# A decoder layer on one core: later loads and stores around job u, key parts a piece later, and one head's probabilities scaled by ScalarE

## The chip, the core and the metric

The kernel runs on one core of a Trainium2 chip. The core has a matrix engine (TensorE, PE in the profile; its weight loads are PEld), VectorE (DVE), ScalarE (ACT), GpSimd (POOL) and SyncE (SP). Each engine takes its instructions from its own queue in the order in which the program gives them. Transfers between the chip's memory and the core's buffer are issued here by SP (the weights and inputs) and by POOL (all else), and run on 16 shared DMA engines. The metric is the time of one execution on the device in microseconds (us), smaller is better, as the median of several runs.

## The reference

One layer of a decoder over 512 positions of 2048 channels, in float32:

```python
h = rms_norm(x, norm_g[l])
proj = h @ w_in[l]
q, kv, g_logits, z_a, uv, z_b, merge_logits = jnp.split(proj, SPLIT_IDX, axis=-1)
o_a = nsa_attention(q, k_c, v_c, k_s, v_s, k_w, v_w, g_logits, ...) * jax.nn.silu(z_a)
o_b = spatial_gating(uv, ln_v_g[l], ln_v_b[l], sgu_w[l], sgu_b[l]) * jax.nn.silu(z_b)
g_a, g_b = jnp.split(jax.nn.sigmoid(merge_logits), 2, axis=-1)
merged = g_a * (o_a @ w_up_a[l]) + g_b * (o_b @ w_up_b[l])
x = x + merged @ w_out[l]
x = x + jax.nn.sigmoid(x @ w_ple_gate[l]) * (p[l] @ w_ple[l])
```

The attention has 16 heads in 4 groups and three branches (compressed, selected, window), each a softmax with a linear bias, weighted by a sigmoid gate and added. With 512 positions the selected and the window branch both see all earlier positions. The gating mixer is `u * (tril(W_s) LN(v) + b)`, with `u` and `v` the two halves of `gelu(uv)`. A final RMS norm follows.

## The kernel before

**Products in three parts.** Every float32 operand of a matrix product is held as a high part (rounded by ScalarE, `high`, L142 and L144) and a low part (the remainder, formed by VectorE, `low`, L148 and L150). A product is three matmuls: high by high, high by low, low by high. So every weight tile that SP loads is first cast by ScalarE (tiles `hi`, `hs`), then subtracted by VectorE (`lo`, `ls`).

**The stream.** All products with weights are jobs in one list. A generator, `gemm`, gives out their matmuls bit by bit. `fill(n)` takes n steps of it, `finish(name)` runs it until a job is done. A step is three matmuls in most jobs; four steps make a piece (one entry of `subs`, one half of a loaded weight tile or one whole one). At the start of a piece the generator runs `flush()`, which carries out what was put into the list `deferred` (what such an entry puts there itself waits for the next flush), then casts and subtracts weights two pieces ahead (`split_to`), then takes from the list `background` as many entries as `state["pops"]` allows (`pop`). An evacuation of a finished product (`job.evac`) comes at the end of its last piece. So the order of each engine's queue is set by the order of these calls in the program.

**Jobs k.** `evac_k` copies a finished 128x512 product of keys out of PSUM: four half-height copies by ScalarE into `ob_h`, four subtractions by VectorE into `ob_l` (L488 to L492).

**The attention.** It is a loop over 48 slots and three more turns to drain it (L1271). For each pair of heads `ft` there are six slots: for the 128-row blocks i = 3 and i = 2 of the queries one slot per branch, for i = 1 and i = 0 one slot with both branches. A slot passes through four stages in four turns: `scores` (matmuls into the two `s` banks; VectorE adds the bias and takes the extreme, L1103; ScalarE's exponentials come two flushes later, L1112), `weigh` one turn later (VectorE: reciprocal L1121, times the gate L1123, and a scaling of each head's probabilities L1127), `transpose_probs` another turn later (TensorE turns up to four 128x128 blocks at a time into one of two `t` banks; ScalarE casts them to `pth`, VectorE subtracts `ptl`), and `values` a turn after that. All but a first group of transposes and of values come at the end of the turn. Between these events the stream is filled in, `per_period` steps a turn; `weigh` is followed by neither a flush nor a fill of its own. Jobs q and za run in the stream here. When the attention is over, its pools are closed, and only then can the pool `quad`, which holds the weights of the next jobs, be filled.

**Job u.** Its product is done by a scheme that saves one of eight block products. With the blocks of the weights named b11, b12, b21, b22, the seven partial products are "1", "2", "5", "6", "3", "7", "4", in this order, "6" and "3" by turns, four pieces each, 28 pieces in all. "1", "6", "7" and "4" share one pair of PSUM banks and add up there. Behind "1", "5" and "6" the state of the banks is copied to tiles `keep` by ScalarE (L656); behind "2", "7" and "3" VectorE adds the banks to such a tile (L667), and after the gelu of `final_u` the tile goes to memory (`u_d`). "6", "5" and "3" read sums of h made earlier: those for "5" and "6" are in `ob_h` and `ob_l`, those for "3" come from `hsum_dram["3"]` (2 MB) and the difference for "7" from `h3_dram` (2 MB, into halves of `act_h` and `act_l` that are free by then). POOL loads both just ahead of job u (L1325, L1328).

**Beside u.** The weights of the spatial gating are turned by TensorE inside u: `wn` (two tiles) and the bias `bn`, both loaded by SP (L1428, L1429), then one transposition of the bias (L1436) and eight of the weights (L1442), after 12, 16 and 20 steps of u. Then `oa_chunk` runs in the background of u and of the next job, vn, four times: two gated attention rows (`oa_f`) are loaded, split into `oa_g0` and `oa_g1`, summed and differenced, and stored to `oa_d` as the seven operands of a later product of the same kind.

Of the kernel before, what the change touches and what calls it, by code (L numbers as in the profile page):

```python
# [21 lines left out]
P = 128  # L22
# [42 lines left out]
def kernel(ctx: ExitStack, tc: tile.TileContext, x, p, norm_g, w_in,  # L65
# [418 lines left out]
    def evac_k(b, a):  # L484
        def f(ps):
            g0, g1 = kk(b, 2 * a), kk(b, 2 * a + 1)
            lo_r, up_r = slice(0, 64), slice(64, 128)
            for dst, srow, g in ((lo_r, lo_r, g0), (up_r, up_r, g1), (up_r, lo_r, g0), (lo_r, up_r, g1)):  # L488
                nc.scalar.copy(ob_h[dst, g], ps[srow])
            for dst, srow, g in ((lo_r, lo_r, g0), (up_r, up_r, g1), (up_r, lo_r, g0), (lo_r, up_r, g1)):  # L490
                nc.vector.tensor_tensor(out=ob_l[dst, g], in0=ps[srow], in1=ob_h[srow, g].bitcast(F32),
                                        op=ALU.subtract)  # L492
        return f
# [152 lines left out]
    def evac_quad(final, place=None, tiles=True):  # L646
# [4 lines left out]
        def e(p, ps):  # L651
            if p in "156":
                tag, pool, bufs = {"1": ("s1", quad["pool"], 2), "5": ("hi", stream, 4), "6": ("lo", stream, 3)}[p]
                keep[p] = [pool.tile([P, 512], F32, tag=tag, name="keep" + p, bufs=bufs) for _ in range(2)]
                for t in range(2):
                    nc.scalar.copy(keep[p][t], ps[t])  # L656
            elif p in "372":
                other, row, c = {"3": ("6", 0, 512), "7": ("5", 2, 512), "2": ("1", 0, 0)}[p]
                for t in range(2):
# [8 lines left out]
                    later(lambda o=o, t=t: final(row + t, c, o, o))  # L668
            else:
# [28 lines left out]
    add_job(Job("u", "S", w_in, C_UV, 512, KT, part_act, evac_quad(final_u), ("s", "g", "t"), order=("1", "2", "5", "63", "7", "4")))  # L698
# [418 lines left out]
    def weigh(s):  # L1117
# [6 lines left out]
        for hh in range(2):  # L1124
            for j in range(nb):
                sl = pts[hh][:, j * n:j * n + n]
                nc.vector.tensor_scalar(out=sl, in0=sl, scalar1=st[:, 0, j, hh:hh + 1], scalar2=None, op0=ALU.mult)  # L1127
# [137 lines left out]
    credit, per_period = 0.0, (phase_b_units - 19 - 8) / (n + 3)  # L1265
# [45 lines left out]
    tmp_pool.update(p=mix["pool"], n=2, tag="v")  # L1311
    load_next()
    finish("za7")
# [9 lines left out]
    sums_of["3"] = [new_s4(q) for q in range(2)]  # L1323
    for q in range(2):
        nc.gpsimd.dma_start(sums_of["3"][q], hsum_dram["3"][:, 4 * q:4 * q + 4])  # L1325
    for i, a in enumerate((act_h, act_l)):
        for q in range(2):
            nc.gpsimd.dma_start(a(slice(4 * q, 4 * q + 4), slice(256, 512)), h3_dram[:, 4 * q:4 * q + 4, 256 * i:256 * i + 256])  # L1328

    def oa_chunk(c):  # L1330
# [8 lines left out]
        def put(n, places, sl=slice(0, 512)):  # L1339
# [475 lines left out]
```

## Time and profile before

| | |
|---|---|
| median of three runs | 1582.59 us (1582.2 to 1583.36) |
| the profiled execution | 1583.81 us, span 1582.1 us |
| TensorE busy | 1548.1 us, 98% |
| VectorE busy | 1194.5 us, 76% |
| ScalarE busy | 786.6 us, 50% |
| GpSimd busy | 252.6 us, 16% |
| moved by DMA | 269.23 MB, mean 170 GB/s |

The profile shows one execution. Its rows give, for an instruction or a group, the start, the time, the engine, the line of the kernel and the tiles written and read (`out<-in`); what stands in brackets is how long the engine had stood idle before and what ended that. A view of the waits adds these up by what was waited for. Slices are the 40 equal parts of the span (39.6 us each), a digit is the busy share in tenths. A matmul of 512 columns is shown as 0.39 us, but matmuls overlap: the distance between two starts is the time that one takes. The jobs k lie at about 90 to 136 us, the attention at 223 to 490 us, job u at 499 to 598 us.

### The profile page before, as it was taken

Reading aid. Unit: us, or ns where it says so; the run is one execution under the profiler, and the core shown is the slowest. Engines: PE = TensorE matmul, PEld = TensorE weight load, DVE = VectorE, ACT = ScalarE, POOL = GpSimd, SP = SyncE. Lnnn points to the kernel's source line nnn. Section 1 sums busy time; section 2 is a strip of 40 time slices with the busy share of each in tenths; the row PEclk is TensorE's granted clock in tenths of the full one; section 3 lists DMA queues with packets and bytes.
Section 4 is the critical chain, followed back from the end, with each engine's and each line's share of the span. In section 5 each row is a group of like instructions: output and inputs, shape, how many; then the busy total and the mean of one; then the engine's idle time right before and its main releaser. Section 6 shows DMA issues by size and latency. Waiting matters only on the chain.

```text
span 1582.1 us, 20502 instructions
## 1 busy us (share of the span) xinstructions
PE 1548.1 (98%) x7438; PEld 1292.7 (82%) x7438; DVE 1194.5 (76%) x1869; ACT 786.6 (50%) x1343; POOL 252.6 (16%) x408
## 2 busy tenths in 40 slices
PE   9999999999999889999999999999999999999997
PEld 8888988888887678888888888888888888888886
DVE  6556758879895677978887778787757587888877
ACT  6434446666663345554554444445423343544555
POOL 1201101101123123300221121211113121000100
PEclk9999999999999899999999999999999999999999
DMA  9425721113315775735473646486552369454555
GB/s 324 121 80 181 224 75 54 51 51 100 87 55 176 256 232 174 235 111 186 149 270 131 227 132 232 169 287 239 206 193 93 115 211 300 147 186 173 183 199 190
DMA packets 162309, 269.23 MB, mean 170 GB/s; under 512 B 9736, under 2 KB 81056, under 8 KB 159648
## 3 DMA queue, kind: packets, MB, share of 16 engines
q1 hardware_dynamic: 117312, 152.20, 29.6%
q0 software_dynamic: 44752, 115.47, 21.7%
q8 instruction: 58, 0.95, 0.2%
q14 instruction: 43, 0.35, 0.1%
q10 hardware_dynamic: 144, 0.26, 0.0%
HBM read 209.69 MB, written 58.20 MB: 169 GB/s over the span
## 4 chain that ended last, share of the span: by engine, by line
PE 88%; DVE 5%; DMA 2%; ACT 2%; issue 2%; POOL 1%; SPq 0%; DVEq 0%; POOLq 0%; ACTq 0%
PE ps_m L336 6%; PE ps_m L337 6%; PE ps_m L338 6%; PE ps_ub L376 2%; PE ps_wo L375 2%; PE ps_wo L376 2%; PE ps_wo L374 2%; PE ps_ub L374 2%; PE ps_ub L375 2%; PE ps_wo L337 2%; PE ps_wo L336 2%; PE ps_wo L338 2%; PE ps_pg L338 2%; PE ps_ua L338 2%; PE ps_ua L336 2%
## 5 line engine op out<-in xcount | busy, mean ns | idle before, releaser
L148 DVE TENSOR_TENSOR ls<-b,hs 128x1024 fp32r<-128x1024 f32 x196 | 239.8, 1224 | 117.6 <-ACT hs L142 116.7
L142 ACT CAST hs<-b 128x1024 fp32r<-128x1024 f32 x196 | 205.7, 1051 | 230.7 <-PE ps_m L338 86.4
L148 DVE TENSOR_TENSOR lo<-raw,hi 128x512 fp32r<-128x512 f32 (+1 forms) x216 | 151.4, 707 | 82.5 <-issue 19.7
L142 ACT CAST hi<-raw 128x512 fp32r<-128x512 f32 (+1 forms) x216 | 129.7, 608 | 137.7 <-PE ps_ub L376 48.5
L142 ACT CAST hs<-raw 128x1024 fp32r<-128x1024 f32 x80 | 84.1, 1053 | 90.1 <-PE ps_m L338 35.5
L148 DVE TENSOR_TENSOR ls<-raw,hs 128x1024 fp32r<-128x1024 f32 x80 | 97.8, 1222 | 14.9 <-ACT hs L142 14.6
L336 PE MATMUL ps_m<-hs,act_h 128*128 128x512 f32 x256 | 100.5, 392 | 0.0
L337 PE MATMUL ps_m<-ls,act_h 128*128 128x512 f32 x256 | 99.7, 389 | 0.0
L338 PE MATMUL ps_m<-hs,act_l 128*128 128x512 f32 x256 | 99.7, 389 | 0.0
L245 DVE TENSOR_TENSOR b<-b,b 128x1024 f32<-128x1024 f32 x80 | 97.5, 1218 | 1.1 <-DMA b<-in_w_in_dram 1.1
L245 DVE TENSOR_TENSOR b<-raw,b 128x1024 f32<-128x1024 f32 x80 | 97.4, 1218 | 0.0
L1112 ACT ACTIVATE prob<-prob,st 128x512 f32<-128x512 f32 (+3 forms) x128 | 70.7, 555 | 17.3 <-DVE st L1103 17.3
L142 ACT CAST pth<-ps_t 128x512 fp32r<-128x512 f32 (+1 forms) x88 | 47.7, 544 | 50.3 <-PE ps_t L1151 49.9
L148 DVE TENSOR_TENSOR ptl<-ps_t,pth 128x512 fp32r<-128x512 f32 (+1 forms) x88 | 55.7, 638 | 19.2 <-ACT pth L142 18.7
L1103 DVE CUSTOM_DVE_ANT_0 prob<-ps_s,b 128x512 f32<-128x512 f32 (+3 forms) x128 | 56.3, 486 | 6.2 <-PE ps_s L1100 5.7
L338 PEld LDWEIGHTS ps_m<-hs,act_l 128*128 128x128 f32 x256 | 48.1, 188 | 10.1
L336 PEld LDWEIGHTS ps_m<-hs,act_h 128*128 128x128 f32 x256 | 48.1, 188 | 9.8
L337 PEld LDWEIGHTS ps_m<-ls,act_h 128*128 128x128 f32 x256 | 48.1, 188 | 9.6
L362 PE MATMUL ps_za<-act_h,hi 128*128 128x512 f32 x128 | 55.0, 430 | 0.0
L362 PE MATMUL ps_q<-act_h,hi 128*128 128x512 f32 x128 | 54.0, 422 | 0.0
L1151 PEld LDWEIGHTS ps_t<-ident,prob 128*128 128x128 f32 x320 | 39.7, 140 | 13.6 <-DVE ptl L148 2.3
L364 PE MATMUL ps_za<-act_h,lo 128*128 128x512 f32 x128 | 50.4, 394 | 0.0
(635 smaller groups left out, 4406.4 us busy)
## 6 DMA issues: line engine op xcount, KB each, us to landing
raw<-in_w_in_dram SPq DMA_DIRECT2D x112, 512.0 KB, 3.6
b<-in_w_in_dram SPq DMA_DIRECT2D x56, 512.0 KB, 5.3
raw<-in_w_out_dram SPq DMA_DIRECT2D x24, 512.0 KB, 3.6
raw<-in_w_ple_gate_dram SPq DMA_DIRECT2D x24, 512.0 KB, 3.8
raw<-in_w_up_b_dram SPq DMA_DIRECT2D x16, 512.0 KB, 3.6
oa_d<-oa_g POOLq DMA_DIRECT2D x56, 128.0 KB, 2.5
hsum<-h_stage POOLq DMA_DIRECT2D x12, 512.0 KB, 3.7
gate<-keep POOLq DMA_DIRECT2D x24, 256.0 KB, 3.7
```

The lines of the kernel that those rows point to most:

```text
L142: nc.scalar.copy(hi, src)
L148: nc.vector.tensor_tensor(out=lo, in0=src, in1=hi.bitcast(F32), op=ALU.subtract)
L245: nc.vector.tensor_tensor(out=b[o], in0=b[x], in1=b[y], op=ALU.subtract)
L336: nc.tensor.matmul(o, ah, wh, start=st, stop=False, skip_group_check=go)
L337: nc.tensor.matmul(o, ah, wl, start=False, stop=False, skip_group_check=go)
L338: nc.tensor.matmul(o, al, wh, start=False, stop=sp, skip_group_check=go)
L362: nc.tensor.matmul(ps, hi[:, j], ah, start=st, stop=False)
L374: nc.tensor.matmul(o, ah[:, sl], hi[:, j], start=st, stop=False)
L375: nc.tensor.matmul(o, ah[:, sl], lo[:, j], start=False, stop=False)
L376: nc.tensor.matmul(o, al[:, sl], hi[:, j], start=False, stop=sp)
L1103: nc.vector.tensor_tensor_reduce(out=pt[:, j * n:j * n + n], in0=o[:, j], in1=b0[:, 512 - n:], scale=-SLOPE[h], scalar=3.0e38, op0=ALU.add ...
L1112: nc.scalar.activation(sl, sl, AF.Exp, bias=st[:, 0, j, hh:hh + 1], scale=-1.0, accum_out=st[:, 1, j, hh:hh + 1])
```

## The change

There are six edits, made together.

1. `evac_k` puts its four VectorE subtractions off: two to the next flush, two to the one after.
2. `weigh` scales only the first head's probabilities on VectorE; the second head's are scaled by ScalarE (`nc.scalar.mul`) in a function put into `deferred`.
3. The attention takes two more steps of the stream (`- 19 - 6` for `- 19 - 8` over all turns).
4. `wn`, `ws`, `tri` and `bn` are set up right after the attention and `wn` and `bn` are loaded by POOL; the last gate's tile `zt` comes from the tag `hs` of `quad` (three tiles) in place of `v` of `mix` (two tiles).
5. The loads of `hsum_dram["3"]` and `h3_dram` move into a hook, `u_then`, behind the evacuations of "1" and of "2". A POOL copy of one column out of the `keep` tile stands ahead of each, so that the loads are issued after that tile is written.
6. In u, the bias is turned after 20 steps in place of 12, and the oa chunks so begin two pieces later, at 1.25 pops a piece in place of 1.15. A chunk has 15 entries in place of 13, four empty ones between its load and its first `put`. `put` takes its tiles by name: both `g0` and `g1`, or one of them for the high part with the low part in its other half or in the loaded tile itself. The low part and the stores come in the flush after the high part; before, the stores came one flush later still.

The diff, cut to its core:

```diff
@@ evac_k
-            for dst, srow, g in ((lo_r, lo_r, g0), (up_r, up_r, g1), (up_r, lo_r, g0), (lo_r, up_r, g1)):
-                nc.vector.tensor_tensor(out=ob_l[dst, g], in0=ps[srow], in1=ob_h[srow, g].bitcast(F32),
-                                        op=ALU.subtract)
+            def lows(i):
+                for dst, srow, g in todo[i]:
+                    nc.vector.tensor_tensor(out=ob_l[dst, g], in0=ps[srow], in1=ob_h[srow, g].bitcast(F32),
+                                            op=ALU.subtract)
+                if i == 0:
+                    deferred.append(lambda: lows(1))
+            deferred.append(lambda: lows(0))
@@ u_then
+    def u_then(p, o):
+        if p not in "12":
+            return
+        nc.gpsimd.tensor_copy(small[:, 72:73], o[:, 0:1])
+        if p == "1":
+            sums_of["3"] = [new_s4(q) for q in range(2)]
+            for q in range(2):
+                nc.gpsimd.dma_start(sums_of["3"][q], hsum_dram["3"][:, 4 * q:4 * q + 4])
+        else:
+            for i, a in enumerate((act_h, act_l)):
+                for q in range(2):
+                    nc.gpsimd.dma_start(a(slice(4 * q, 4 * q + 4), slice(256, 512)),
+                                        h3_dram[:, 4 * q:4 * q + 4, 256 * i:256 * i + 256])
@@ weigh
-        for hh in range(2):
-            for j in range(nb):
-                sl = pts[hh][:, j * n:j * n + n]
-                nc.vector.tensor_scalar(out=sl, in0=sl, scalar1=st[:, 0, j, hh:hh + 1], scalar2=None, op0=ALU.mult)
+        for j in range(nb):
+            sl = pts[0][:, j * n:j * n + n]
+            nc.vector.tensor_scalar(out=sl, in0=sl, scalar1=st[:, 0, j, 0:1], scalar2=None, op0=ALU.mult)
+
+        def second():
+            for j in range(nb):
+                sl = pts[1][:, j * n:j * n + n]
+                nc.scalar.mul(sl, sl, st[:, 0, j, 1:2])
+        deferred.append(second)
@@ the attention's loop
-    credit, per_period = 0.0, (phase_b_units - 19 - 8) / (n + 3)
+    credit, per_period = 0.0, (phase_b_units - 19 - 6) / (n + 3)
@@ after the attention
-    tmp_pool.update(p=mix["pool"], n=2, tag="v")
+    tmp_pool.update(p=quad["pool"], n=3, tag="hs")
     load_next()
...
+    for hf in range(2):
+        nc.gpsimd.dma_start(wn[hf], sgu_w[4 * hf:4 * hf + 4].rearrange("g t s -> t g s"))
+    nc.gpsimd.dma_start(bn, sgu_b)
     finish("za7")
@@ oa_chunk, put
-                split(h, l, w[n][:, sl], 0.5, later=True)
-                def store():
...
-                later(store)
+                h = mix["pool"].tile([P, S], F32R, tag=tags[0], name="oa_" + tags[0])
+                if len(tags) == 2:
+                    l = mix["pool"].tile([P, S], F32R, tag=tags[1], name="oa_" + tags[1])
+                else:
+                    l = w[n].bitcast(F32R) if width == 512 else h[:, 256:]
+                high(h[:, :width], w[n][:, sl], 0.5)
+                def rest():
+                    low(h[:, :width], l[:, :width], w[n][:, sl], 0.5)
...
+                deferred.append(rest)
-        return [load, nothing, nothing, put("2", (5, 6)), nothing, nothing, put("1", (0,), lo_t), sums_13, sums_24,
-                put("1", (2, 4)), nothing, nothing, put("2", (3, 1))]
+        return ([load] + 4 * [nothing] + [put("2", ("g0", "g1"), (5, 6))] + 3 * [nothing]
+                + [put("1", ("g0",), (0,), lo_t), sums_13, sums_24, put("1", ("g1",), (2, 4)), nothing, put("2", ("g0",), (3, 1))])
@@ beside u
-    state["pops"] = 1.15
-    fill(12)
+    state["pops"] = 1.25
+    fill(20)
```

More of the change, by code (lines that the diff above doesn't have):

```diff
@@ L656, in e @@
                     nc.scalar.copy(keep[p][t], ps[t])
+                if then:
+                    then(p, keep[p][1])
             elif p in "372":
@@ L668, in e @@
                     later(lambda o=o, t=t: final(row + t, c, o, o))
+                if then:
+                    then(p, keep[other][1])
             else:
@@ L1321, in new_s4 @@
         return t
[L1323 to L1328, printed above, removed]
     def oa_chunk(c):
```

22 lines of the change are left out of this document (10 added, 12 removed).

## The prediction

> **What bounds the kernel now.** I read the page's slices first, then the waits of TensorE, then its timeline around each wait, and last the rows of VectorE and ScalarE in the attention.
>
> ```profile
> span 1582.1 us, 20502 instructions
> ...
> PE   9999999999999889999999999999999999999997
> ...
> PEclk9999999999999899999999999999999999999999
> ```
> TensorE is the bound: only two slices (514 to 593 us, job u) are below nine tenths, and there the granted clock dips as well. The waits of TensorE say where to look:
>
> ```profile
> PE ps_u L336 <- ACT hs L142: 6.1, 1, 6.1
> PE ps_u L336 <- DVE keep L667: 4.7, 1, 4.7
> PE ps_b L1436 <- DMA sum<-in_sgu_b_dram: 2.4, 1, 2.4
> PE ps_k L364 <- DVE lo L148: 1.9, 1, 1.9
> ```
> Each wait costs more than itself, since the matmuls behind it run at half pace for a while. So I price a wait by the matmul starts on its two sides (first column: start):
>
> ```profile
> 127.04 0.39 PE L363 MATMUL ps_k<-act_l,hi 128*128 128x512 f32 x1
> ...
> 133.28 0.39 PE L362 MATMUL ps_k<-act_h,hi 128*128 128x512 f32 x1
> ...
> 508.50 0.39 PE L338 MATMUL ps_u<-hi,act_l 128*128 128x512 f32 x1
> ...
> 515.62 0.40 PE L338 MATMUL ps_u<-hi,act_l 128*128 128x512 f32 x1
> ...
> 535.66 0.39 PE L338 MATMUL ps_u<-hs,ob_h 128*128 128x512 f32 x1
> ...
> 546.64 0.39 PE L336 MATMUL ps_u<-hs,ob_h 128*128 128x512 f32 x1
> ...
> 579.74 0.39 PE L338 MATMUL ps_u<-hs,act_l 128*128 128x512 f32 x1
> ...
> 591.04 0.39 PE L336 MATMUL ps_u<-hs,act_h 128*128 128x512 f32 x1
> ...
> 598.30 0.39 PE L338 MATMUL ps_u<-hs,act_l 128*128 128x512 f32 x1
> ```
> The last two rows give the pace: 32 matmuls in 7.26 us, 0.227 us each. The four stretches hold 11, 12, 10 and 16 matmuls, so they lose 6.24 - 2.50 = 3.7 (job k), 7.12 - 2.72 - 0.12 for the small transposition = 4.3 (ps_b), 10.98 - 2.27 = 8.7 (behind ScalarE) and 11.30 - 3.63 = 7.7 us (behind keep): 24.4 us in all, of which 15.1 are the waits and 9.3 the slow pace behind them.
>
> What stands behind the waits:
>
> ```profile
> 124.54 2.80 DVE L491 TENSOR_TENSOR ob_l<-ps_k,ob_h 64x512 fp32r<-64x512 f32 x4 [3.08 <-ACT ob_h L489]
> ```
> ```profile
> 498.99 4.21 SPq L1428 DMA_DIRECT2D wn<-in_sgu_w_dram  x2
> 503.25 2.03 SPq L1429 DMA_DIRECT2D sum<-in_sgu_b_dram  x1
> ```
> ```profile
> 521.26 1.08 POOL L1337 DMA_DIRECT2D oa_f<-o_d  x2
> ```
> ```profile
> 538.04 0.63 ACT L144 ACTIVATE oa_g<-oa_f 128x512 fp32r<-128x512 f32 x1 [9.02 <-DMA oa_f<-o_d]
> ```
> ```profile
> 580.61 0.42 DVE L150 SCALAR_TENSOR_TENSOR oa_g<-oa_f,oa_g 128x256 fp32r<-128x256 f32 x1 [2.64 <-DMA oa_d<-oa_g]
> ...
> 584.01 1.28 DVE L667 TENSOR_TENSOR keep<-ps_u,keep 128x512 f32<-128x512 f32 x2
> ```
> In job k, four subtractions (2.80 us) stand on VectorE ahead of the low part of the next weights. The bias table is issued only at 503.25, behind tiles still in use. The first attention rows, issued at 521.26, are there only at 538.04, and ScalarE, which takes its work in order, holds the weights' cast behind them. And VectorE stands 2.64 us before a tile that a store still reads, so the keep additions come late.
>
> **The change, part by part.** *evac_k*: the subtractions come two by two, a piece later, so the next low part is 1.4 us earlier, and the staged sums that were queued behind them use VectorE's 3.08 us of waiting for the ScalarE copies. I take all of it: -3.7 (ends 0 and -3.7).
>
> *Early tables*: wn and bn leave SP for POOL, three issues right after the attention and well over 10 us ahead of use; the wait goes: -4.3 (ends 0 and -4.3). SP, no longer stopped at 498.99 to 505, still has to wait for a free raw tile for its next load.
>
> *Attention rows*: their load is issued two pieces of u later and cast five pops behind it instead of three, at 1.25 pops a piece instead of 1.15. That is four pieces (48 matmuls, 10.9 us) instead of about two and a half. But the four h3 loads (2 MB) now stand just ahead of it on POOL, the hsum loads come after the first evacuation. 16.8 us from issue to cast would still be late, by 10.9 plus the two pieces of ScalarE's lead (5.5) = 16.4, by 0.4 us; with the 2 MB of hsum out of the way I count on less. The two small POOL copies that hold these loads back wait for the last keep instruction of "1" and of "2"; queued behind them on POOL are the loads, the two ws stores, the attention rows and u's own stores, and only the rows have a reader that is near. hsum is first read by piece 14 of u and h3 by piece 21, some 27 us (10 pieces of 2.7) and 35 us behind their new places. -8.7, and +1 for new short waits here and at the first b12 load (ends 0 and +8.7, the old wait kept).
>
> *Places of the parts*: two of the four low parts go into the loaded tile itself, and no oa work falls into the last piece before "4". The next chunk's load then waits on POOL for the store out of that tile, with u's stores behind it; four empty pops cover it, so nothing. The last gate's zt takes one of the three hs tiles, which u first needs at its fifth piece: nothing. What is left is that "4" writes the banks that the keep addition reads, with no piece between: an addition of 0.64 us (half of 1.28), partly under the last matmuls; I take 0.4. -7.7 + 0.4 = -7.3 (ends -7.7 and 0).
>
> *Two more steps of the stream inside the attention* (six matmuls) leave 1.4 us less TensorE work to cover the first load of u, which cannot start before the attention's pools are free:
>
> ```profile
> 498.21 0.39 PE L364 MATMUL ps_za<-act_h,lo 128*128 128x512 f32 x1
> 499.20 0.50 PE L336 MATMUL ps_u<-hi,act_h 128*128 128x512 f32 x1 [0.60 <-ACT hi L142]
> ```
> The work is only moved, but the gap of 0.76 (0.99 less one matmul) becomes 2.1 us, as long as that of ps_b, and I take its slow pace as well: 4.3 less the gap of 2.55 is +1.7 (ends 0 and +3.1, that and the 1.4). The Trainium skill, "TensorE: Matmul & The Clock Gate", section "HAM oscillation — how this bites in real kernels", has gaps over about 3.4 us as those that throttle; by it this term would be 0 and the sum 1.7 less. The rows behind 127.04 differ: there a wait of 1.9 us was enough, and the measurement decides.
>
> *The second head on ScalarE* is the part that decides. One slot of the attention, VectorE and then ScalarE:
>
> ```profile
> 215.00:490.00 275.00, 270.14 (x1513) 227.49 (x1512) 231.29 (x692) 179.50 (x479) 42.72 (x70) 1.00 0.21 62
> ```
> ```profile
> 251.73 0.69 DVE L1103 CUSTOM_DVE_ANT_0 prob<-ps_s,b 128x512 f32<-128x512 f32 x1 [0.40 <-PE ps_s L1100]
> ...
> 253.17 0.16 DVE L1123 TENSOR_TENSOR st<-st,gates 128x4 f32<-128x4 f32 x1
> 253.36 0.88 DVE L1127 TENSOR_SCALAR prob<-prob,st 128x128 f32<-128x128 f32 x4
> 254.16 0.68 DVE L148 TENSOR_TENSOR ptl<-ps_t,pth 128x512 fp32r<-128x512 f32 x1
> 255.62 0.69 DVE L148 TENSOR_TENSOR ptl<-ps_t,pth 128x512 fp32r<-128x512 f32 x1 [0.78 <-ACT pth L142]
> ...
> 257.78 0.69 DVE L1103 CUSTOM_DVE_ANT_0 prob<-ps_s,b 128x512 f32<-128x512 f32 x1
> ```
> ```profile
> 252.69 0.59 ACT L142 CAST pth<-ps_t 128x512 fp32r<-128x512 f32 x1 [1.89 <-PE ps_t L1151]
> 253.18 0.73 ACT L1112 ACTIVATE prob<-prob,st 128x512 f32<-128x512 f32 x1
> ...
> 253.89 0.71 ACT L1112 ACTIVATE prob<-prob,st 128x512 f32<-128x512 f32 x1
> ...
> 255.00 0.59 ACT L142 CAST pth<-ps_t 128x512 fp32r<-128x512 f32 x1 [0.30 <-PE ps_t L1151]
> ```
> VectorE loses half of 0.88, some 21 us over 48 slots, of 231 busy in 275. ScalarE has room for 64 scalings at no more than a cast's 0.59 each. So by busy time the move costs nothing. By order it does. The scaling is put aside and runs at the next flush, ahead of the first pth cast and of the exponentials of the slot, and both engines take their work in order. It needs st of L1123, which VectorE has only at 253.33, behind the slot's two reductions. So ScalarE would do: scaling from 253.38 to about 253.83 (two of 128 columns; I take 0.45, from a cast's 0.59), pth until 254.32 (0.49 from start to start, 252.69 to 253.18), and the exponentials from there instead of from 253.18, 1.14 later. The second pth had 0.40 of slack (from the end of the last exponential, 253.89 + 0.71, to 255.00), so it comes 0.74 later, with it the second ptl, and behind that on VectorE the next slot's reduction at 257.78. That reduction leads to the next st, so the delay is paid again: it is a ring through both engines, with 253.17 to 257.78 and on as one turn. TensorE waits when the reductions, which free its score banks, are a slot behind. Behind the scaling on ScalarE stand the weights' casts too, and VectorE's low parts wait for those. In 8 of the 48 slots the probabilities that are turned have a single cast, and the reduction doesn't stand behind a second one; 40 slots at 0.74 are +30. The ends: -4.9 (TensorE's whole idle time, 275.0 - 270.1, goes because VectorE is freer) and +55 (1.14 in each of 48).
>
> The sum: 1583.8 (the profiled execution's time, 1.7 over its span) - 3.7 - 4.3 - 8.7 + 1 - 7.3 + 1.7 + 30 = 1592.5. The median of the runs shown is 1.2 below the profiled execution: 1591.
>
> **The rivals.** *The scaling hides, so it is faster.* ScalarE is idle for 95 of the 275 us, much of it before pth, as the 1.89 above; if TensorE stays the slower partner and the ring keeps slack, the attention keeps its time or gains up to 4.9. Then 1583.8 - 21.3 - 1.2 = 1561, less at best 1556. This case holds if a turn of the ring grows by under 0.45 us on 40 slots (18 us, with which the sum comes to 1580). The Trainium skill, "Perfetto Trace Analysis", section "Optimizing Scalar/DVE Operations", speaks for it: with VectorE saturated, giving work to ScalarE may pay. Against it: VectorE is 84% busy here, and the row of 255.62 shows it waiting for ScalarE's pth already.
>
> *The ring in full.* Each slot pays 1.14, or gaps in the attention slow the clock as the 1.9 us of job k did: 1583.8 - 21.3 + 55 - 1.2 = 1616. For it: other work (casts, folds) also stands in the ring; against it: TensorE's own slack.
>
> *Half and half.* The ring costs 15 to 20, or u keeps one of its waits while the scaling hides: around 1579. Here the two halves of the change cancel.
>
> **How the numbers follow.** The ring as forecast, 1583 to 1600: 0.45. Hidden, 1556 to 1564: 0.25. Half and half, 1572 to 1584: 0.18. In full, about 1616: 0.12. The time is that of the first, 1591. The range leaves out half of the hidden case and most of the last: 1561 to 1608. The first alone would be 1583 to 1600. What a measurement can tell from no change is about 0.2%, 3.2 us, so 1579.4 to 1585.8 is the same: 0.10, from the low edge of the first and the middle of the third case. Faster: 0.25 and 0.08 of the third = 0.33. Slower: the rest, 0.57.
>
> **What the profile would show.** If I am right, the four waits at the top are gone or under 1 us, the slices of u are at nine, and the slices of the attention (220 to 500 us) fall to eight, with TensorE waiting at ps_s or ps_c for VectorE's L1103, and the stretch of the attention some 30 us longer with 21 us less VectorE work. If the scaling hides, the attention's stretch keeps its 275 us. I am wrong in u if a wait for oa_f, b or keep of over 2 us is there, and wrong at its start if the gap before its first matmul isn't about 2 us.

## The result and the profile after

| | before | after |
|---|---|---|
| median of 4 runs | 1582.39 us (1582.13 to 1583.36) | 1609.5 us (1608.26 to 1611.27) |
| after / before | | 1.0171, 95% interval 1.0153 to 1.0189 |
| span of the profiled execution | 1582.1 us | 1608.3 us |
| VectorE busy | 1194.5 us | 1178.2 us |
| ScalarE busy | 786.6 us | 814.2 us |

The change makes the kernel 27 us slower, where +8.6 was forecast. In the changed kernel the lines of the attention have moved: the reduction is L1128 (L1103 before), the exponentials L1137 (L1112), the product with the gate L1148 (L1123), the scalings L1151 on VectorE and L1156 on ScalarE (L1127), the transposes L1181 (L1151), the keep additions L675 (L667).

The page of the changed kernel: span, two rows of slices, two groups (busy time, mean ns of one, then the idle time ahead of them and what ended it).

```profile
span 1608.3 us, 20489 instructions
...
PE   9999998889989999999999999999999999999997
...
PEclk9999999999999999999999999999999999999999
...
L148 DVE TENSOR_TENSOR ptl<-ps_t,pth 128x512 fp32r<-128x512 f32 (+1 forms) x88 | 56.3, 643 | 74.0 <-ACT pth L142 73.7
...
L1156 ACT ACTIVATE prob<-prob,st 128x512 f32<-128x512 f32 (+3 forms) x64 | 34.2, 558 | 85.1 <-DVE st L1148 84.9
```

The slices of u (14 to 16) are at nine now, those of the attention (7 to 9 and 12) at eight. ScalarE stands 84.9 us in all ahead of the scalings, waiting for the gate product, and VectorE's ptl waits 73.7 us for pth. The waits of TensorE in the changed kernel say the same (total, times, longest):

```profile
PE ps_t L1181 <- DVE ptl L148: 8.6, 10, 1.8
PE ps_s L1124 <- ACT pct L1275: 5.7, 3, 3.2
PE ps_c L1283 <- DVE st L1128: 5.0, 4, 1.8
PE ps_c L1273 <- DVE st L1128: 4.2, 3, 3.2
PE ps_s L1124 <- ACT cs L1246: 3.4, 2, 1.9
PE ps_s L1124 <- DVE st L1128: 3.4, 2, 2.1
PE ps_u L336 <- ACT hi L142: 2.1, 2, 1.4
...
PE ps_u L337 <- DVE ls L148: 1.3, 2, 0.7
PE ps_u L336 <- DVE keep L675: 1.3, 1, 1.3
PE ps_pg L392 <- DVE tl L148: 1.0, 2, 0.8
PE ps_pg L337 <- DVE ls L148: 1.0, 2, 0.8
```

All four waits that headed this view before (hs 6.1, keep 4.7, the bias table 2.4, lo 1.9) are gone or shrunk to 1.3. The new ones lie in the attention, and two small ones in pg, the last job. From the first to the last ps_s the two kernels compare like this (stretch, then busy time of PE, PEld, DVE, ACT and POOL, the granted clock, the DMA share and GB/s); first before:

```profile
223.34:476.99 253.65, 248.79 (x1400) 209.37 (x1398) 215.68 (x651) 169.11 (x452) 36.98 (x61) 1.00 0.22 65
```

and after:

```profile
218.69:515.69 297.00, 265.02 (x1405) 215.27 (x1404) 200.83 (x590) 193.58 (x506) 35.59 (x61) 0.97 0.20 56
```

The attention takes 43.3 us more, with 14.9 us less work on VectorE. TensorE's idle time there goes from 4.9 to 32.0 us, and it is busy for 16.2 us longer (granted clock 0.97 in the mean); some 1.4 us of that are the six matmuls of the two more steps.

The stretches add up to the result. From the first ps_k to the first ps_vs: 55.03 to 50.98, -4.1. The attention: +43.3. From the last ps_za to the first ps_vn, which is u: 100.31 to 85.01, -15.3. From the first to the last ps_pg: 164.8 to 168.5, +3.7. Together +27.6; the rest of the program gives 1.4 back, and the spans differ by 26.2.

### The profile page after: what moved, and what is told of

The parts are those of the page before. It is cut to its first block, busy times and chain, and to the rows that moved or that the text cites. A ratio compares the mean times of both kernels' runs of the same rounds, so it can differ in the third digit from the quotient of the medians.

```text
span 1608.3 us, 20489 instructions
## 1 busy us (share of the span) xinstructions
PE 1555.9 (97%) x7438; PEld 1291.2 (80%) x7438; DVE 1178.2 (73%) x1805; ACT 814.2 (51%) x1407; POOL 257.2 (16%) x413
## 4 chain that ended last, share of the span: by engine, by line
PE 78%; DVE 9%; ACT 7%; issue 3%; DMA 2%; POOL 1%; DVEq 0%; ACTq 0%; SPq 0%; POOLq 0%
PE ps_m L336 6%; PE ps_m L337 6%; PE ps_m L338 6%; ACT prob L1137 3%; DVE prob L1128 2%; PE ps_ub L375 2%; PE ps_ub L376 2%; PE ps_wo L374 2%; PE ps_wo L376 2%; PE ps_wo L375 2%; PE ps_ub L374 2%; PE ps_wo L336 2%; PE ps_ua L338 2%; PE ps_ua L337 2%; PE ps_zb L337 2%
## 5 line engine op out<-in xcount | busy, mean ns | idle before, releaser
L148 DVE TENSOR_TENSOR lo<-raw,hi 128x512 fp32r<-128x512 f32 (+1 forms) x216 | 151.9, 708 | 79.9 <-issue 20.5
L148 DVE TENSOR_TENSOR ptl<-ps_t,pth 128x512 fp32r<-128x512 f32 (+1 forms) x88 | 56.3, 643 | 74.0 <-ACT pth L142 73.7
L1156 ACT ACTIVATE prob<-prob,st 128x512 f32<-128x512 f32 (+3 forms) x64 | 34.2, 558 | 85.1 <-DVE st L1148 84.9
L1137 ACT ACTIVATE prob<-prob,st 128x512 f32<-128x512 f32 (+3 forms) x128 | 70.6, 555 | 5.6 <-DVE st L1128 5.6
L1181 PEld LDWEIGHTS ps_t<-ident,prob 128*128 128x128 f32 x320 | 40.1, 144 | 25.5 <-DVE ptl L148 14.6
L1181 PE MATMUL ps_t<-ident,prob 128*128 128x128 f32 x320 | 51.6, 281 | 8.8 <-DVE ptl L148 8.6
L1128 DVE CUSTOM_DVE_ANT_0 prob<-ps_s,b 128x512 f32<-128x512 f32 (+3 forms) x128 | 56.3, 486 | 4.7 <-PE ps_s L1125 4.4
```

The source lines that it names most:

```text
L148: nc.vector.tensor_tensor(out=lo, in0=src, in1=hi.bitcast(F32), op=ALU.subtract)
L1128: nc.vector.tensor_tensor_reduce(out=pt[:, j * n:j * n + n], in0=o[:, j], in1=b0[:, 512 - n:], scale=-SLOPE[h], scalar=3.0e38, op0=ALU.add ...
L1137: nc.scalar.activation(sl, sl, AF.Exp, bias=st[:, 0, j, hh:hh + 1], scale=-1.0, accum_out=st[:, 1, j, hh:hh + 1])
L1181: nc.tensor.transpose(b[:, (2 * e + hh) * P:(2 * e + hh + 1) * P], pts[hh][:, c:c + P], ident)
```

## The experiments

Ratios are to the kernel before, run on the same chip each time. The attention column is the stretch from the first to the last ps_s in the profiled execution.

| kernel | median us | ratio (95%) | attention us |
|---|---|---|---|
| before | 1582.4 | 1 | 253.65 |
| after | 1609.5 | 1.0171 (1.0153 to 1.0189) | 297.00 |
| both heads on VectorE, rest as after | 1565.56 | 0.9896 (0.9884 to 0.9909) | 254.80 |
| before, second head on ScalarE | 1621.21 | 1.0241 (1.0227 to 1.0256) | 293.04 |
| scaling behind the exponentials | 1575.64 | 0.9957 (0.9945 to 0.9969) | 263.37 |
| wait alone | 1588.37 | 1.0037 (1.0024 to 1.0050) | 277.77 |
| work alone | 1569.14 | 0.9910 (0.9896 to 0.9925) | 257.96 |
| wait alone, behind the exponentials | 1566.47 | 0.9897 (0.9880 to 0.9913) | 255.55 |
| both heads on ScalarE | 1634.53 | 1.0320 (1.0303 to 1.0338) | 321.64 |
| second head on GpSimd | 1563.94 | 0.9876 (0.9862 to 0.9891) | 253.10 |

### The scaling undone, and the scaling alone

The first kernel is the one after with the old loop in `weigh`; the second is the one before with only the new one.

```diff
-        for j in range(nb):
-            sl = pts[0][:, j * n:j * n + n]
-            nc.vector.tensor_scalar(out=sl, in0=sl, scalar1=st[:, 0, j, 0:1], scalar2=None, op0=ALU.mult)
-
-        def second():
-            for j in range(nb):
-                sl = pts[1][:, j * n:j * n + n]
-                nc.scalar.mul(sl, sl, st[:, 0, j, 1:2])
-        deferred.append(second)
+        for hh in range(2):
+            for j in range(nb):
+                sl = pts[hh][:, j * n:j * n + n]
+                nc.vector.tensor_scalar(out=sl, in0=sl, scalar1=st[:, 0, j, hh:hh + 1], scalar2=None, op0=ALU.mult)
```

> The kernel after with one part undone: both heads' probabilities are scaled by VectorE again, the other five edits stay. My theory: the whole cost of the change is the second head on ScalarE, which made the 48 slots 43 us longer (253.6 to 296.9 us from the first to the last ps_s). Then this kernel takes 1609.5 - 43 = about 1566 us, 1563 to 1570, 1% less than the kernel before. Rival: the two more steps in the attention, or the tables loaded early, are part of the 43 us; then it stays above 1572.

> The kernel before with one part of the change alone: the second head scaled by ScalarE at the next flush. If the 43 us belong to this part alone: 1582.4 + 43 = about 1625 us, 1620 to 1630, with the ps_s stretch at about 297 us. If the other parts share in it (two more steps of the stream in the attention, a later start of the first load of u): under 1615.

Both came out as the first theory has it. Without the scaling on ScalarE the rest of the change is a gain of 1% (17 us on medians, 1565.56 against 1582.7); with it alone the loss is 38.5 us (1621.21 against 1582.7). In the kernel after the same edit costs 43.9 (1609.5 less 1565.56). The 5 us between the two are not settled: the attention's stretch grew by 42.2 there and by 39.4 here. The stretch with both heads on VectorE:

```profile
218.72:473.52 254.80, 250.67 (x1405) 210.34 (x1404) 215.71 (x652) 168.95 (x452) 36.01 (x61) 1.00 0.23 65
```

It is 1.15 us longer than before and TensorE is 1.9 us busier: the two more steps of the stream (six matmuls, 1.4 us).

### The place in ScalarE's queue

The kernel after with the scaling one flush later, behind the slot's exponentials:

```diff
-        deferred.append(second)
+        later(second)
```

> The kernel after with the same scaling on ScalarE, put off by one flush more, so that it stands behind the pth cast and the exponentials of the slot in place of ahead of them. If the cost is the place in ScalarE's queue (a wait for st at the head of it, with pth and the exponentials behind): most of the 43 us goes, 1563 to 1575 us, and ScalarE's wait for st ahead of the scaling (84.9 us in all) falls to under 10 us. If the cost is the scaling's own time on ScalarE (34 us busy, which the casts and exponentials must give way to wherever it stands): 1595 to 1610.

1575.64 us, just past the upper end of the first expectation: 10 us over both heads on VectorE in place of 44. The scaling itself takes the same time, and its wait is gone, as the group's row shows:

```profile
L1156 ACT ACTIVATE prob<-prob,st 128x512 f32<-128x512 f32 (+3 forms) x64 | 33.8, 553 | 0.4 <-DVE st L1148 0.4
```

So three quarters of the cost hang on the place. The other quarter is left with the scaling between the exponentials and the second pth.

### Wait and work apart

In both kernels VectorE scales both heads. In the first, ScalarE copies one column of st in the scaling's place; in the second it scales, three times a slot, a small tile that nobody reads and that depends on nothing but ScalarE itself.

```diff
+        deferred.append(lambda: nc.scalar.copy(small[:, 74:75], st[:, 0, 0, 1:2]))
```

```diff
+    scr = att.tile([P, 40], F32, name="scr")
+    nc.gpsimd.memset(scr, 0.0)
...
+        deferred.append(lambda: [nc.scalar.mul(scr, scr, 1.0) for _ in range(3)])
```

> The kernel after with both heads scaled by VectorE, but with a copy of one column of st by ScalarE at the place where the second head's scaling stood: the wait for st at the head of ScalarE's queue without the scaling's 34 us of work. If the wait is the cost: +20 to +40 us over the kernel with both heads on VectorE, 1586 to 1606 us. If the work is the cost: within 6 us of that kernel, about 1570 us.

> Both heads on VectorE as in the kernel with one part undone (1565.6 us), and at the place of the second head's scaling three scalings by ScalarE of a tile of 40 columns that nobody reads: work of about the same time there (an estimated 0.7 us a slot), but no wait for st. If the work costs because the wait has moved it behind st, into the turn of the slot: without the wait it falls into ScalarE's idle time ahead of pth (1.1 to 2.5 us in the rows of that kernel) and costs 0 to 5 us, 1566 to 1571. If the work costs wherever it stands, as the 21 us between the wait alone and the kernel after would have it: 1583 to 1590.

The wait alone costs 22.8 us (1588.37 less 1565.56), the work alone 2.2 (0.9910 less 0.9896, of 1583; the intervals overlap), and the two together in the kernel after 43.9. They don't add up: the remaining 19 us are work that costs only because the wait has put it behind st. ScalarE's rows show how. The row of the pth casts with both heads on VectorE:

```profile
L142 ACT CAST pth<-ps_t 128x512 fp32r<-128x512 f32 (+1 forms) x88 | 47.6, 544 | 51.2 <-PE ps_t L1176 50.7
```

with the work alone, and the work itself:

```profile
L142 ACT CAST pth<-ps_t 128x512 fp32r<-128x512 f32 (+1 forms) x88 | 47.5, 543 | 26.9 <-PE ps_t L1179 26.4
L1155 ACT ACTIVATE scr<-scr 128x40 f32<-128x40 f32 x144 | 34.0, 236 | 3.2
```

and with the wait alone:

```profile
L142 ACT CAST pth<-ps_t 128x512 fp32r<-128x512 f32 (+1 forms) x88 | 47.6, 543 | 2.0 <-PE ps_t L1177 1.5
L1153 ACT COPY small<-st 128x1 f32<-128x1 f32 x48 | 9.1, 190 | 84.8 <-DVE st L1148 84.5
```

With both heads on VectorE, ScalarE stands 51 us ahead of pth, waiting for TensorE's transposes. 34 us of work that is free to start at once fit in there: 24 us of them come out of that standing time. With a wait for st in the same place, pth stands behind VectorE's reductions, always: the wait for ps_t is down to 1.5 us because st comes later than ps_t. Then nothing is left in which work could hide.

### A wait in the later place

> Both heads on VectorE, and ScalarE's one-column copy of st a flush later, behind the exponentials: the wait in the place where the scaling cost 10 us over the kernel with both heads on VectorE. If st is long there by then: 0 to 2 us, 1565 to 1568, and those 10 us were the scaling's time between the exponentials and the second pth. If the wait still holds the second pth: 1570 to 1576.

The same one-column copy of st, `later(...)` in place of `deferred.append(...)`: 0.9897 against 0.9896. The wait costs nothing there, so the 10 us of the scaling in this place are put down to its time, by elimination. That the second head's probabilities are ready later hardly counts: in the kernel with the scaling behind the exponentials, TensorE waits for the scaling only once, 0.2 us, with a weight load of ps_t.

### Twice the work

The kernel after with the first head's scaling in `second` too, and none on VectorE.

> The kernel after with the first head's probabilities scaled by ScalarE too, in the same place: the work there doubles (34 us to 68), the wait for st stays one a slot. If the work adds to the turn of each slot (as 21 of the 44 us between the wait alone and the kernel after suggest): +15 to +35 over the kernel after, 1625 to 1645 us. If the wait at the head of the queue is the whole mechanism, or VectorE's relief of another 20 us counts: 1600 to 1612.

25 us more than the kernel after on medians (24 by the ratios), with one wait a slot as there. The group's row has 63.2 us of work and the same wait:

```profile
L1153 ACT ACTIVATE prob<-prob,st 128x512 f32<-128x512 f32 (+3 forms) x128 | 63.2, 553 | 83.6 <-DVE st L1148 83.4
```

29 us more work on ScalarE cost about 25 us, although VectorE has 22 us less to do in the stretch (200.83 to 178.34). Behind st most of ScalarE's work is paid, and VectorE's relief is worth a few us at most.

### An engine outside the ring

The kernel after with the second head scaled by GpSimd, straight behind the first.

```diff
+                (nc.vector, nc.gpsimd)[hh].tensor_scalar(out=sl, in0=sl, scalar1=st[:, 0, j, hh:hh + 1], scalar2=None, op0=ALU.mult)
```

> The kernel after with the second head scaled by GpSimd instead of ScalarE, right behind the first head's on VectorE. GpSimd is 16% busy and issues neither pth nor exponentials, so by the ring theory the same scaling costs nothing there, or gains a little because VectorE has 20 us less: 1560 to 1567 us, against 1565.6 with both on VectorE. It takes an estimated 0.8 to 1.1 us for 512 columns (its additions of 256 columns take 0.77 to 0.81 us, of 512 columns 1.1 to 1.5), some 50 to 70 us in all. If what costs is that the second head's probabilities are ready later, or that VectorE and GpSimd slow each other: over 1575.

1563.94 us, 0.9876: no loss against both heads on VectorE, though GpSimd is busy 71 us longer for what ScalarE does in 34, and 1757 ns for 512 columns where 0.8 to 1.1 us were estimated (the stretch, then the row of the longest scalings):

```profile
218.76:471.86 253.10, 250.25 (x1406) 210.40 (x1404) 201.27 (x592) 169.11 (x452) 107.51 (x121) 1.00 0.23 66
```

```profile
L1152 POOL TENSOR_SCALAR prob<-prob,st 128x512 f32<-128x512 f32 x16 | 28.1, 1757 | 33.0 <-ACT prob L1137 11.8 <-DVE st L1148 11.6 <-ACT pth L142 6.1
```

The wait for st is in that row too (11.6 us, 67.5 over all four widths). Behind it stand GpSimd's own additions and the stores that it issues, and the attention's stretch is no longer for it. The Trainium skill, "Perfetto Trace Analysis", section "Optimizing Scalar/DVE Operations", says that offloading from VectorE to GpSimd might not help, since they share a read port. A small effect of that kind would fit this trace: VectorE's own 64 scalings take 425 ns in the mean beside GpSimd's, 387 in the kernel after. That the port is the cause is not shown, and it doesn't decide anything here.

### The last job, pg

The wait of ps_pg for ls stands in every kernel above that has the other five edits, and in all but one of them a wait for tl too. The stream's `pop` adds `state["pops"]` to a sum, takes an entry for every whole one and keeps the fraction. With u's pops at 1.25 in place of 1.15, the fraction when pg's entries are put in is 0.6 in place of 0.2, and each entry falls at another piece. One line ahead of pg in the kernel with both heads on VectorE, and the reverse (0.6) in the kernel before:

```diff
     state["pops"] = 0.5
+    state["due"] = 0.2
```

> The kernel with both heads on VectorE and the other five edits, with one line more: the fraction that the stream's pop carries on from job to job (0.2 in the kernel before, 0.6 in this one, since u's pops went from 1.15 to 1.25) is set to 0.2 ahead of the last job, pg. If that fraction, which puts each background entry of pg at another piece, is the cause of the new waits in pg: the stretch from the first to the last ps_pg goes from 171.0 back to 164.8 us, and the time from 1565.6 to about 1560 (1558 to 1562). If a slower arrival of pg's weights or the clock is the cause: no change, 1564 to 1567.

> The kernel before with the fraction set to 0.6 ahead of pg and nothing else. If the fraction is the cause: the waits of ps_pg for tl and ls appear here too, the pg stretch goes from 164.8 to 167 to 171 us, and the time is 1585 to 1589. Else: 1582.5, as before.

The first: 1563.63 us, ratio 0.9870 (0.9856 to 0.9885), above the 1558 to 1562 expected, no wait of ps_pg left, and the pg stretch is 165.4 us in place of 171.0. The second: 1584.86 us, 1.0010 (1.0000 to 1.0019), just under the 1585 to 1589 expected, pg 167.1 us in place of 164.8, with this row among its waits, which the kernel before doesn't have (the wait for tl, expected too, is not there):

```profile
PE ps_pg L337 <- DVE ls L148: 1.0, 2, 0.8
```

So the fraction makes the waits for ls, and in the changed kernels those for tl go with it too. Its price differs from trace to trace: the pg stretch is 167.1 to 171.0 us in the kernels that have it. Part of the difference is the clock: the trace with 171.0 us has a granted clock of 0.50 from 1537.2 to 1540.6 us, behind these waits, and stands for an execution of 1569.19 us, 3.6 above the median of its kernel; that with 168.5, the kernel after, has no such stretch in pg. So the price is better read from the times, 1.9 us on medians and 4 by the ratios; the interval of the second just touches 1.

### The parts of u, one undone each

Both heads on VectorE; in the first the loads of hsum and h3 are ahead of u again and `u_then` is gone, in the second `put` is the old one, in the new list.

> Both heads on VectorE, the other edits stay, but the loads of hsum and h3 (4 MB) are issued ahead of u by GpSimd again, ahead of the attention rows. If the moved loads are what lets the rows come in time: a wait of ps_u of 3 to 6 us for hs behind the rows' cast returns, u is 4 to 9 us longer (85.5 to 90 to 94 us from the last ps_za to the first ps_vn), 1570 to 1575. If the two later pieces and the two more empty pops are enough by themselves: u keeps its 85.5 us, 1565 to 1567.

> Both heads on VectorE, the other edits stay, but put is that of the kernel before: always both tiles, the stores one flush later, in the list of 15 entries. If the tiles and the earlier stores are what removes the wait behind keep (my term of -7.3): VectorE's stand before a tile that a store still reads is back, u is 4 to 8 us longer, 1569 to 1574. If the places in the list do it: no change, 1565 to 1567.

The first: 1568.24 us, 0.9908 (0.9893 to 0.9923), u at 86.4 us in place of 85.5. No wait of ps_u for hs is over 1.3 us: the rows come in time by the later place and the empty pops alone. Moving 4 MB of loads is worth 1 to 2 us at most, not the 4 to 9 expected, and the two intervals overlap. For the rows themselves the move is a loss: on GpSimd they stand behind the moved loads, and ScalarE, which doesn't wait for the first of them here, waits 3.85 us with the loads moved and 3.79 us in the kernel after:

```profile
581.68 0.63 ACT L144 ACTIVATE oa_g<-oa_f 128x512 fp32r<-128x512 f32 x1 [3.79 <-DMA oa_f<-o_d]
```

No wait of TensorE comes of it. The second: 1571.5 us, 0.9924 (0.9910 to 0.9939), inside what the first theory expected, but u is not longer at all (85.2 us). The loss is in zb, 81.4 us in place of 75.9, where the last chunk ends. ScalarE's row there:

```profile
659.24 0.63 ACT L144 ACTIVATE oa_g<-oa_f 128x512 fp32r<-128x512 f32 x1 [5.97 <-DMA oa_d<-oa_g]
```

It stands 5.97 us before a tile that a store still reads, with the weights of zb behind it. So u is cured without the moved loads and without the new `put`, each undone alone; that leaves the places in the list, which no kernel undoes, and the new `put` keeps a like stall from appearing two jobs on.

### Two cures together, and the two steps

Second head on GpSimd and the fraction set to 0.2; then the same with `- 19 - 8` in place of `- 19 - 6`.

> Both cures together: the second head scaled by GpSimd, and the pop's fraction set to 0.2 ahead of pg. If they are independent: the attention stretch at 253 us and the pg stretch at 165 us, 1558 to 1562 us, ratio to the kernel before about 0.985. If either only works beside the other's old state: no better than 0.987.

> The same with the stream's share of the attention as in the kernel before (two steps less in the attention, two more behind it, ahead of u's first load). By my term for this edit (0 to +3.1, taken as +1.7, of which 1.4 is the gap itself and the rest a slow pace that the traces do not show): 1.0 to 1.7 us less than with the two steps, with the gap ahead of the first ps_u shrinking from 2.3 us to about 1. If the two steps pay for themselves in the attention: the same or up to 1 us more.

1561.58 us, 0.9863 (0.9846 to 0.9879), and 1561.46 us, 0.9862 (0.9847 to 0.9877). The first is just inside what was expected and is, with its twin, the fastest kernel of this study: 1.4% under before, 3% under after. Without the two steps 1.0 to 1.7 us less was expected, and 0.1 came. (In the prediction the +1.7 was the slow pace alone, and the 1.4 of the gap stood only in the upper end.) The two steps move about 1 us from one side to the other (from the last ps_za to the first ps_u 2.10 us with, 1.04 without; attention 253.14 with, 252.03 without) and decide nothing. The slow pace that the expectation doesn't find in the traces is in some of them (below).

## Why the prediction was wrong, point by point

**The direction and the mechanism** were right: u and the jobs k gain about what was said, the attention loses more, by the ring through ScalarE and VectorE, and TensorE's waits are at ps_s, ps_c and ps_t. The size of the ring was wrong: +43.3 us in place of +30, and with it the time lies outside the range.

**The step that failed is "40 slots at 0.74", with 8 slots at nothing.** For the slot on which it was worked out it was fair. In the changed kernel the same turn (the weighing of two branches of 128 columns) reads, VectorE first:

```profile
253.06 0.17 DVE L1148 TENSOR_TENSOR st<-st,gates 128x4 f32<-128x4 f32 x1
253.26 0.48 DVE L1151 TENSOR_SCALAR prob<-prob,st 128x128 f32<-128x128 f32 x2
254.51 0.69 DVE L148 TENSOR_TENSOR ptl<-ps_t,pth 128x512 fp32r<-128x512 f32 x1 [0.77 <-ACT pth L142]
256.40 0.69 DVE L148 TENSOR_TENSOR ptl<-ps_t,pth 128x512 fp32r<-128x512 f32 x1 [1.20 <-ACT pth L142]
...
258.56 0.69 DVE L1128 CUSTOM_DVE_ANT_0 prob<-ps_s,b 128x512 f32<-128x512 f32 x1
```

and ScalarE:

```profile
253.32 0.70 ACT L1156 ACTIVATE prob<-prob,st 128x128 f32<-128x128 f32 x2 [2.06 <-DVE st L1148]
253.92 0.56 ACT L142 CAST pth<-ps_t 128x512 fp32r<-128x512 f32 x1
254.38 0.72 ACT L1137 ACTIVATE prob<-prob,st 128x512 f32<-128x512 f32 x1
...
255.10 0.71 ACT L1137 ACTIVATE prob<-prob,st 128x512 f32<-128x512 f32 x1
...
255.81 0.57 ACT L142 CAST pth<-ps_t 128x512 fp32r<-128x512 f32 x1
```

The pair of scalings takes 0.60 from start to start of what follows (253.32 to 253.92), not 0.45. From the gate product to the next slot's reduction it is 5.50 us (253.06 to 258.56), against 4.61 before (253.17 to 257.78): +0.89, where +0.74 was said. But this turn is one of six kinds. From one slot's reciprocal to the next, means of eight in the profiled executions (seven for the first kind, whose turn the first slot lacks), named by the slot that the interval ends at:

| interval ends at | before | both on VectorE | wait alone | after | both on ScalarE |
|---|---|---|---|---|---|
| i = 3, first branch (the turn above) | 6.27 | 6.19 | 6.36 | 6.79 | 7.37 |
| i = 3, second branch (single cast) | 4.75 | 4.56 | 5.19 | 5.58 | 6.12 |
| i = 2, first branch | 5.88 | 6.00 | 6.35 | 6.91 | 7.50 |
| i = 2, second branch | 5.12 | 5.25 | 6.11 | 6.43 | 6.97 |
| i = 1 | 4.66 | 4.21 | 5.33 | 5.69 | 6.13 |
| i = 0 | 5.46 | 6.19 | 6.10 | 6.70 | 7.22 |

From before to after the priced kind pays 0.52, the least of all; the others pay 0.83 to 1.31, the turn with a single cast, put down at nothing, 0.83 too. Over the 47 intervals that is 47.2 us (the stretch of ps_s, cut at other ends, grew by 43.3): 6.6 from the single-cast turns in place of nothing, 36.9 from the four other kinds where 0.74 makes 23.7, and 3.6 from the priced kind where it makes 5.2. The wait falls unevenly (from about 0 to 1.12, wait alone against both on VectorE), the work evenly (0.3 to 0.6, after against the wait alone, and as much again with both heads). The rows explain the unevenness in two turns. With both heads on VectorE ScalarE starts the first pth of the next turn well before st is there (rows of the timeline, ScalarE's first, then VectorE's):

```profile
248.72 0.59 ACT L142 CAST pth<-ps_t 128x512 fp32r<-128x512 f32 x1 [2.52 <-PE ps_t L1176]
...
254.05 0.59 ACT L142 CAST pth<-ps_t 128x512 fp32r<-128x512 f32 x1 [1.57 <-PE ps_t L1176]
```

```profile
248.52 0.16 DVE L1148 TENSOR_TENSOR st<-st,gates 128x4 f32<-128x4 f32 x1
...
254.82 0.29 DVE L1148 TENSOR_TENSOR st<-st,gates 128x2 f32<-128x2 f32 x1
```

There pth runs 1.06 us ahead of st (254.05 against 254.82 + 0.29). In the wait alone the same pth starts 0.18 us behind st (258.26 against 257.78 + 0.30), and the interval, one of the second kind, takes 6.9 us in place of 5.7. In the priced kind of turn the kernel with both heads on VectorE has pth at 248.72, behind st at 248.68: nothing to lose. That the other four kinds differ by the same reason is likely from the table and not shown row by row.

**The slow pace.** In the prediction each wait of job k and u was priced with the half pace behind it, but the ring's 30 us were a sum of delays alone, and a slower clock in the attention was left to the rival "in full". After, TensorE's idle time in the stretch is up by 27.1 us and its busy time by 16.2 us, 1.4 of it for six more matmuls. The granted clock is 0.50 in five short stretches, 20.5 us in all; this row lies in the longest of them:

```profile
268.30:275.10 6.80, 5.32 (x16) 4.07 (x17) 4.58 (x12) 4.14 (x11) 2.67 (x5) 0.50 0.17 43
```

Whether the slow matmuls lengthen the ring's turns or only fill time in which TensorE would have stood idle was not tried. The traces speak for the second in the main: in this stretch ScalarE and VectorE together wait for TensorE for 14.7 us, against 65.3 before (ahead of pth 0.4 us, against 46.7), so the ring hardly waits for matmuls any more.

**The rivals.** In this place the scaling does not hide; work that waits for nothing does, as the work alone shows. "In full" gave 1616 by 1.14 in each of 48 slots; the stretch makes it 0.90 (43.3 over 48), and u and pg gained 6 us less than that sum had. The rule of the Trainium skill that was named for the first rival ("Perfetto Trace Analysis", "Optimizing Scalar/DVE Operations": with VectorE saturated, giving work to ScalarE may pay) did not come true here, with VectorE 84% busy before: VectorE lost 19 us of scaling (42.5 to 23.4 us, where 21 were said) and the time went up.

**Job k**: -3.7 forecast, -4.1 measured. **u with its start**: -4.3 - 8.7 + 1 - 7.3 + 1.7 = -17.6 forecast, -15.3 measured; the waits that remain are hi 1.4 and 0.7, ls 1.3 and keep 1.3, where under 1 us was said for keep. Two steps in it were credited to the wrong edit: the rows come in time without the moved loads of hsum and h3, and TensorE's wait for keep is down to 1.5 us without the new `put` too, which does its work in zb. One sign of being wrong, a wait for oa_f of over 2 us, is there, on ScalarE (3.79 us): the rows are issued 34.5 us behind the first ps_u, 12.5 later than before, where two pieces (5.5 us) were said. They then take 8.2 us to the cast in place of 16.8. The gap at the start of u is near what was forecast (2.1 us, a matmul taken off; here 1.83 from start to start, so 1.60), in TensorE's timeline:

```profile
537.17 0.39 PE L364 MATMUL ps_za<-act_h,lo 128*128 128x512 f32 x1
539.00 0.50 PE L336 MATMUL ps_u<-hi,act_h 128*128 128x512 f32 x1 [1.44 <-ACT hi L142]
```

but the slow pace behind it is not in this trace. The granted clock of the 10 us after it is 1.00, and of the stretch with job k's wait of 1.9 us, before, it was 0.73. Here is the row of u's start:

```profile
539.00:549.00 10.00, 8.86 (x35) 6.55 (x36) 6.36 (x10) 5.60 (x10) 2.60 (x5) 1.00 1.05 404
```

and that of job k before the change:

```profile
127.00:133.30 6.30, 4.43 (x13) 3.15 (x13) 5.42 (x9) 1.27 (x3) 1.53 (x3) 0.73 0.60 180
```

Other kernels with the same two steps do show it: with both heads on VectorE the 10 us behind the first ps_u are

```profile
495.58:505.58 10.00, 9.78 (x35) 7.72 (x36) 6.26 (x10) 5.44 (x9) 2.98 (x5) 0.83 1.05 403
```

It costs little there, since the same 35 matmuls fill time in which TensorE otherwise waits for weights: u takes 85.5 us, against 85.1 in the same kernel with the fraction set, where the clock is 1.00. The term of +1.7 is not borne out: without the two steps the time was 0.1 us lower.

**Unforeseen**: +3.7 in pg, with waits made by a fraction of a counter that the changed pops of u leave behind.

By these terms: 0.4 less for k, 13.3 more for the attention, 2.3 for u, 3.7 for pg, 18.9 in all on a forecast of +8.7 for the profiled execution; that makes 27.6, which the other stretches bring down to 26.2.

## What to carry to other kernels

Moving work to an idle engine that takes its instructions in order costs the instruction's wait as well as its time, and the wait is paid by what stands behind it: ask which of those could have started earlier, and price them in every kind of turn, not in the one that lies open on the screen. Where the work must wait for a late value, put it behind what doesn't need that value, or on an engine whose queue holds nothing urgent, even if that engine is slower. And when a schedule carries a fraction on from stage to stage, a changed rate in one stage moves the places in all later ones: fix the fraction at the stage's start.

## What the runs showed of the hardware

GpSimd's scaling of 128x512 takes 1757 ns by its row and ScalarE's 722 ns, yet the slower engine gives the faster kernel. ScalarE's scalings by form in the changed kernel:

```profile
L1156 ACT ACTIVATE prob<-prob,st 128x512 f32<-128x512 f32 x16 | 11.5, 722 | 24.1 <-DVE st L1148 24.0
L1156 ACT ACTIVATE prob<-prob,st 128x384 f32<-128x384 f32 x16 | 9.9, 616 | 35.3 <-DVE st L1148 35.1
L1156 ACT ACTIVATE prob<-prob,st 128x256 f32<-128x256 f32 x16 | 7.3, 502 | 12.1 <-DVE st L1148 12.1
L1156 ACT ACTIVATE prob<-prob,st 128x128 f32<-128x128 f32 x16 | 5.5, 394 | 13.7 <-DVE st L1148 13.7
```

A quarter of the columns takes more than half of the time, so two of 128 columns, which the prediction priced below one cast of 512, take about as long as one scaling of 512 (the pair above 0.70 us from start to end, against 0.722). The 512 columns are also over the 0.59 us that the prediction set as the most for one scaling. And a wait of TensorE has no fixed price in clock. Behind a stop of 1.9 us in job k the granted clock was 0.50 from 129.85 to 133.2 us, with 0.43 us from one matmul to the next in place of 0.23. At the start of u the same 2.10 us between the last ps_za and the first ps_u left it at 1.00 in one kernel (both heads on VectorE, fraction 0.2) and at 0.83 over the next 10 us in another (second head on GpSimd, fraction 0.2). And 28 waits of up to 3.2 us in the attention took it to 0.97 in the mean.
